# A fused attention layer on Trainium2: the per-layer embedding product computed before attention and kept in DRAM

## The chip, the core and the metric

The kernel runs on one core of one Trainium2 chip. A core has a matrix engine (PE, with its weight loads listed apart as PEld), a vector engine (DVE), a scalar engine (ACT), a general engine (POOL) and a queue engine that only issues transfers (SP). Each runs its own instruction list in order; they meet at semaphores. SP and POOL issue the transfers, which 16 DMA engines carry. The metric is the device time of one execution in microseconds, lower is better.

## What is computed

One layer over 512 tokens of width 2048. Cut to what matters here:

```python
hn = rmsnorm(x, norm_g)                            # 512 x 2048
x = x + swa_mixer(hn, w_in, w_out, sinks, rel_bias)  # windowed attention, 32 heads of 64, gated
emb = p @ ple_proj                                 # 512 x 256 times 256 x 2048
g = sigmoid(rmsnorm(x, ple_norm) @ ple_gate)       # 512 x 2048 times 2048 x 2048
x = x + emb * g
out = rmsnorm(x, final_g)
```

`p` and `ple_proj` are inputs: `emb` depends on nothing that the layer computes.

## The kernel before

Every float32 product is made of three matmuls on numbers split into a high and a low part (`mm3`, lines 123 to 128: high by high, high by low, low by high). A weight tile of 128x1024 arrives as `wraw` or `braw`, ACT makes the high part from it (`whi`, `bhi`), DVE the low part (`wlo`, `blo`). That pair of instructions is called a split below. Raw tiles and both parts have three buffers each.

The stages in order of time. **First projections** (lines 199 to 309): k, v and the first two q tiles. **Attention** (lines 852 to 941): 64 steps of softmax work, one every 5.6 us, between which PE makes the remaining 30 q and gate tiles. The generator `projections` yields after each product of three matmuls, seven or eight products fall into a step, and class `Weights` keeps its splits a few tiles ahead through a list `todo`, emptied at fixed points of a step. In the same steps `sum_weights` (line 686) prepares sums of weight blocks in DRAM for the later stages: SP issues a plain copy DRAM to DRAM (line 689), POOL later adds a second block into it (line 691). The first eight copies are issued at the end of step 0 (`sums_in`, line 883). **Output product** (lines 1107 to 1153) and **gate stage** (from line 1157): both use a Strassen scheme of seven half-size products, named by p, in two halves jj; class `Pieces` loads and splits their weight tiles. PE runs the gate stage in the order p = 2, 7, 1, 6, 5, 3, 4. The embedding is made there: for p = 1, 5, 3 each half loads a piece of `ple_proj` ("proj", split like a weight tile), and after the half's 48 matmuls `embed` (line 1165) makes two banks with six matmuls each; p = 4 is made block by block by `block` (line 1299, tiles named `last`), each block followed by six embedding matmuls, the last block in two halves of 256 columns. `gated` (line 1171) then multiplies the sigmoid with the embedding bank, adds to x and squares.

Order of the engines: PE and SP follow the program text everywhere. DVE, ACT and POOL do so from line 340 until the end of attention and again from the second product of the gate stage on (line 1258); between them a scheduler orders them. So code that is written elsewhere is issued elsewhere, and an instruction that waits holds up all behind it on its engine.

Of the kernel before, what the change touches and what calls it, by code (L numbers as in the profile page):

```python
# [55 lines left out]
def trunk_kernel(ctx: ExitStack, tc: tile.TileContext, a: dict):  # L56
# [31 lines left out]
    class Weights:  # L88


        def __init__(self, ahead):
            self.srcs, self.ahead, self.raw, self.made = [], ahead, [], []

            self.todo, self.asked, self.apart = [], 0, False

        def add(self, src):
            self.srcs.append(src)
# [1 line left out]
        def load(self, upto):  # L99
            for i in range(len(self.raw), upto):  # L100
                self.raw.append(wpool.tile([P, WE], F32, tag="wraw", name=f"wraw{i}"))
                nc.sync.dma_start(self.raw[i], self.srcs[i])

        def _make(self, i):
            self.load(min(i + 2, len(self.srcs)))
            raw = self.raw[i]
            hi = wpool.tile([P, WE], F32R, tag="whi", name=f"whi{i}")
            lo = wpool.tile([P, WE], F32R, tag="wlo", name=f"wlo{i}")
            nc.scalar.copy(hi, raw)  # L109
            nc.vector.tensor_sub(lo, raw, hi.bitcast(F32))  # L110
            self.made.append(tuple(t.rearrange("p (k c) -> p k c", k=8) for t in (hi, lo)))
# [77 lines left out]
    for kind, c in kinds:  # L189
# [470 lines left out]
    def block(nm, r, c, jj, m):  # L660
        return a[nm][2 * (c - 1) + jj, 4 * (r - 1) + m]

    SUMS = [("w_out", 7), ("w_out", 5), ("w_out", 6), ("w_out", 4), ("ple_gate", 7), ("ple_gate", 5)]

    def small_block(r, c, m):
# [27 lines left out]
    class Pieces:  # L693
# [9 lines left out]
        def _prepare(self, i):  # L703
            kind, src, key = self.specs[i]
            if kind == "grow":
                t = self.grown[key]
                nc.gpsimd.dma_start(t, src, accum_op=ALU.add)  # L707
            else:
                if kind == "seed":
# [10 lines left out]
                nc.sync.dma_start(t.rearrange("p (k c) -> p k c", k=2) if kind == "proj" else t, src)  # L720
            self.base[i] = t

        def _split(self, i):
            raw = self.base.pop(i)
            hi = wpool.tile([P, WE], F32R, tag="whi", name=f"bhi{i}")
            lo = wpool.tile([P, WE], F32R, tag="wlo", name=f"blo{i}")
            nc.scalar.copy(hi, raw)  # L727
            nc.vector.tensor_sub(lo, raw, hi.bitcast(F32))  # L728
            self.made[i] = tuple([t[:, :512], t[:, 512:]] for t in (hi, lo))
# [36 lines left out]
    def add_stage(nm, order):  # L766
        at = {}

        def add_embeds(p, jj):
            if nm == "ple_gate" and p in (1, 5, 3, 4):  # L770
                j = jj + 2 * (p in (5, 3))
# [80 lines left out]
    def projections():  # L852
        parts = {}
        for m, (kind, c) in enumerate(kinds):

            while any(v in chores for v in parts.get(m - 2, ())):
                chores.pop(0)()
            ps = bank(f"{kind}ps{c}", "p")
            for k in range(KC):
                if m == len(kinds) - 1 and k % 8 == 0:  # L860
                    B.ahead(k // 8 - 2)
                if m == len(kinds) - 1 and 2 <= k:
                    next(first_form, None)
                wh, wl = W.get(2 * m + k // 8)
# [8 lines left out]
    nc.scalar.mul(sinkb, sinkb, -1.0)  # L873
    proj = projections()
    load_bias(0)
    W.apart = True
    for n in range(KC):
        next(proj)
        if n % 4 == 3 and W.todo:
            W.todo.pop(0)()  # L880
    blocks = TWOS * UNITS

    def sums_in(i):
# [67 lines left out]
    pTh = late.tile([P, 2, S], F32R, name="pTh")  # L951
    pTl = late.tile([P, 2, S], F32R, name="pTl")
    ssq2 = const.tile([P, NB, 4], F32, name="ssq2")
    ssq3 = const.tile([P, NB, 5], F32, name="ssq3")

# [200 lines left out]

    rstd2 = const.tile([P, NB], F32, name="rstd2")
    ss2 = const.tile([P, NB], F32, tag="sums", name="ss2")
    pT = wpool.tile([P, WE], F32, tag="wraw", name="pT").rearrange("p (k t) -> p k t", k=2)
    nc.sync.dma_start(pT, a["pT"])  # L1160
    nc.scalar.copy(pTh, pT)
    nc.vector.tensor_sub(pTl, pT, pTh.bitcast(F32))
    done = {t: 0 for t in range(NB)}

    def embed(t, w, tag, c=slice(0, 512)):
        e_ps = bank(f"e{t}_{done[t]}", tag)
        for k in range(2):
            mm3(e_ps[:, c], pTh[:, k, blk(t)], pTl[:, k, blk(t)], w[0][k][:, c], w[1][k][:, c], k == 0, k == 1)
        return e_ps

    def gated(t, j, zin, z, e_ps, c=slice(0, 512)):


        n = done[t]
# [1 line left out]
        xt = x1[j][:, t, c]  # L1176
        nc.scalar.activation(z, zin, AF.Sigmoid, scale=rstd2[:, t : t + 1])
        yield
        nc.vector.tensor_mul(z, e_ps[:, c], z)
        if t >= 2 and j >= 2:  # L1180
            nc.gpsimd.dma_start(xt, z, accum_op=ALU.add)
        else:
# [72 lines left out]
    for n, p in enumerate(ORDER_PLE[:-1]):  # L1255
# [8 lines left out]
        for jj in range(2):  # L1264
# [31 lines left out]
    w = [B.get(at_ple["e", jj]) for jj in range(2)]  # L1296
    f = ple_forms.made[4]

    def block(jj, tb, tag, e_tag, c=slice(0, 512)):

        ps = bank(f"last{jj}_{tb}_{c.start}", tag)
        for k in range(8):
            fh, fl = f[k // 2]
            bh, bl = B.made[at_ple[4, jj][k // 2]]
            mm3(ps[:, c], fh[:, k % 2, blk(tb)], fl[:, k % 2, blk(tb)], bh[k % 2][:, c], bl[k % 2][:, c], k == 0, k == 7)
        e_ps = embed(2 + tb, w[jj], e_tag, c)
        z = s2[:, jj, tb, c]

        def opened():
            nc.vector.tensor_sub(z, ps[:, c], z)  # L1310
            return gated(2 + tb, jj, z, z, e_ps, c)

        return opened

# [14 lines left out]
    g = block(0, 0, "s", "o")()  # L1329
    run(root)  # L1330
    for step in moved.pop():
        step()
# [6 lines left out]
    for j in range(4):  # L1339
        row(1, j, yn2[:, 1:2])  # L1340
        store(1, j)
    g = block(1, 0, "s", "t")()
    next(g)
    for j in (2, 3):
        by_gain(2, j)
# [7 lines left out]
    g = block(0, 1, "p", "o")()  # L1353
    run(root)
    next(g)
    for j in range(2):
# [10 lines left out]
    g = block(1, 1, "p", "t", slice(0, 256))()  # L1367
    next(g)
    by_gain(3, 0)
    next(g)  # L1370
    run(g)
    n = done[3]
    last = block(1, 1, "s", "o", slice(256, 512))()
    next(last)

    nc.vector.tensor_reduce(base, ssq3[:, 3, :n], axis=AX.X, op=ALU.add)
# [83 lines left out]
```

## Time and profile before

| what | value |
|---|---|
| median of 3 runs | 794.62 us (794.57 to 794.85) |
| the profiled execution's own time | 794.82 us |
| span from its first to its last instruction | 793.1 us |
| PE busy | 783.2 us, 99% |
| DVE, ACT, POOL busy | 585.7, 506.7, 148.5 us |
| mean granted clock of PE | 0.997 |
| moved by DMA | 185.23 MB |

The rows of a timeline have the start in us from the span's beginning, the duration, engine, line, operation, the tile written and the tiles read, the shape, and in brackets how long the engine was idle before it and what ended that. A matmul's listed duration overlaps the next one's, so the distance between two starts is what PE spends on one. A row of a table by stretches has the stretch, its length, the busy time of PE, PEld, DVE, ACT and POOL with their counts, the granted clock, the DMA engines' busy share and GB/s.

### The profile page before, as it was taken

How to read it: one execution, taken by the hardware profiler on the slowest of the kernel's cores; microseconds unless marked ns; L12 is line 12 of the kernel's file. 1: busy time of each engine (PE TensorE's matmuls, PEld its weight loads, DVE VectorE, ACT ScalarE, POOL GpSimd, SP SyncE). 2: the span in 40 equal slices, each digit the busy share in tenths (PEclk: the TensorE clock that was granted, in tenths of full speed). 3: DMA queues.
4: the chain of work that ended last, by engine and by line, in shares of the span. 5: the costliest groups of instructions: out<-in, count | busy, mean ns of one | idle time of the engine just before them, and what ended most of it. 6: DMA issues, size and time to landing. Idle time of an engine off the chain costs nothing.

```text
span 793.1 us, 11181 instructions
## 1 busy us (share of the span) xinstructions
PE 783.2 (99%) x3746; PEld 656.0 (83%) x3746; DVE 585.7 (74%) x1155; ACT 506.7 (64%) x1067; POOL 148.5 (19%) x248
## 2 busy tenths in 40 slices
PE   9999999999999999999999999999999999999995
PEld 8888888888888888888888888888888888888885
DVE  4547587867867587767777899778866757988896
ACT  6743576666767586766666654466699656656765
POOL 0200423242413324132324200000000120210000
PEclk9999999999999999999999999999999999999998
DMA  9977999897989989898987498667864996787533
GB/s 349 275 215 264 207 275 303 223 267 215 277 227 269 223 249 258 230 247 235 244 227 182 140 365 337 197 212 232 275 237 142 346 203 202 157 225 220 176 107 106
DMA packets 45066, 185.23 MB, mean 234 GB/s; under 512 B 6656, under 2 KB 7680, under 8 KB 39888
## 3 DMA queue, kind: packets, MB, share of 16 engines
q1 hardware_dynamic: 36928, 143.30, 53.0%
q0 software_dynamic: 8080, 41.22, 27.1%
q8 instruction: 29, 0.48, 0.2%
q14 instruction: 29, 0.24, 0.1%
HBM read 177.63 MB, written 62.97 MB: 303 GB/s over the span
## 4 chain that ended last, share of the span: by engine, by line
PE 99%; DVE 0%; ACT 0%; ACTq 0%; issue 0%; DVEq 0%
PE gps L126 7%; PE gps L127 7%; PE gps L128 7%; PE qps L126 7%; PE qps L127 7%; PE qps L128 7%; PE o L127 6%; PE g L128 6%; PE g L127 5%; PE o L126 5%; PE o L128 5%; PE g L126 5%; PE s L477 2%; PE o L583 2%; PE vps L290 2%; PE pt L541 2%
## 5 line engine op out<-in xcount | busy, mean ns | idle before, releaser
L728 DVE TENSOR_TENSOR blo<-braw,bhi 128x1024 fp32r<-128x1024 f32 x102 | 124.4, 1222 | 40.9 <-ACT bhi L727 40.6
L727 ACT CAST bhi<-braw 128x1024 fp32r<-128x1024 f32 x102 | 107.3, 1052 | 72.2 <-PE o L128 24.8
L126 PE MATMUL gps<-xh,whi 128*128 128x512 f32 x256 | 100.0, 390 | 0.0
L127 PE MATMUL gps<-xl,whi 128*128 128x512 f32 x256 | 99.9, 390 | 0.0
L128 PE MATMUL gps<-xh,wlo 128*128 128x512 f32 x256 | 99.8, 390 | 0.0
L126 PE MATMUL qps<-xh,whi 128*128 128x512 f32 x224 | 87.8, 392 | 0.0
L127 PE MATMUL qps<-xl,whi 128*128 128x512 f32 x224 | 87.4, 390 | 0.0
L128 PE MATMUL qps<-xh,wlo 128*128 128x512 f32 x224 | 87.3, 390 | 0.0
L110 DVE TENSOR_TENSOR wlo<-wraw,whi 128x1024 fp32r<-128x1024 f32 x60 | 73.7, 1229 | 6.1 <-ACT whi L109 5.9
L547 DVE TENSOR_TENSOR r<-pt,r 128x256 fp32r<-128x256 f32 x64 | 27.2, 424 | 66.5 <-ACT r L546 65.6
L546 ACT CAST r<-pt 128x256 fp32r<-128x256 f32 x64 | 23.9, 373 | 80.9 <-PE pt L541 80.8
L126 PE MATMUL g<-bhi,fhg 128*128 128x512 f32 x192 | 75.1, 391 | 0.0
L126 PE MATMUL o<-bhi,fho 128*128 128x512 f32 x192 | 74.8, 390 | 0.0
L128 PE MATMUL g<-bhi,flg 128*128 128x512 f32 x192 | 74.8, 389 | 0.0
L127 PE MATMUL o<-blo,fho 128*128 128x512 f32 x192 | 74.8, 389 | 0.0
L128 PE MATMUL o<-bhi,flo 128*128 128x512 f32 x192 | 74.7, 389 | 0.0
L127 PE MATMUL g<-blo,fhg 128*128 128x512 f32 x192 | 74.7, 389 | 0.0
L557 POOL TENSOR_SCALAR_AFFINE_SELECT own<-r 64x512 fp32r<-64x512 f32 (+1 forms) x48 | 32.5, 677 | 224.6 <-DVE r L547 208.7
L109 ACT CAST whi<-wraw 128x1024 fp32r<-128x1024 f32 x60 | 62.2, 1039 | 5.4 <-issue 4.0
L492 POOL COPY t<-sinkb 128x2 f32<-128x2 f32 x64 | 53.2, 839 | 57.7 <-ACT sinkb L873 32.4
L707 POOL DMA_DIRECT2D grown<-in_ple_gate x16 | 13.8, 861 | 231.0 <-DVE blo L728 226.7
L128 PEld LDWEIGHTS gps<-xh,wlo 128*128 128x128 f32 x256 | 48.1, 188 | 10.3
(228 smaller groups left out, 1800.3 us busy)
## 6 DMA issues: line engine op xcount, KB each, us to landing
wraw<-in_w_gate_in SPq DMA_DIRECT2D x32, 512.0 KB, 6.5
w_out<-in_w_out POOLq DMA_DIRECT2D x32, 512.0 KB, 8.0
braw<-w_out SPq DMA_DIRECT2D x32, 512.0 KB, 4.4
wraw<-in_w_q SPq DMA_DIRECT2D x28, 512.0 KB, 5.3
braw<-in_ple_gate SPq DMA_DIRECT2D x24, 512.0 KB, 4.1
braw<-in_w_out SPq DMA_DIRECT2D x22, 512.0 KB, 4.2
xw<-in_first SPq DMA_DIRECT2D x14, 640.5 KB, 6.4
w_out<-in_w_out SPq DMA_DIRECT2D x16, 512.0 KB, 10.1
```

Of the source, the lines that this page charges most:

```text
L109: nc.scalar.copy(hi, raw)
L110: nc.vector.tensor_sub(lo, raw, hi.bitcast(F32))
L126: nc.tensor.matmul(ps, sh, mh, start=first, stop=False, skip_group_check=more)
L127: nc.tensor.matmul(ps, sh, ml, start=False, stop=False, skip_group_check=more)
L128: nc.tensor.matmul(ps, sl, mh, start=False, stop=last, skip_group_check=more)
L290: nc.tensor.matmul(v_ps[t], h[:, c], part_of(high_at, 256, 512), start=f, stop=e, skip_group_check=True)
L492: nc.gpsimd.tensor_copy(two(0, W + W - 1 if late else W, 1), sinkb[:, d : d + 1].unsqueeze(1).to_broadcast([P, 2, 1]))
L546: nc.scalar.copy(rh, src)
L547: nc.vector.tensor_sub(rl, src, rh.bitcast(F32))
L557: nc.gpsimd.affine_select(out=flat(own), in_=flat(r).bitcast(F32), pattern=[[0, 8], [sign, HB]], compare_op=ALU.is_ge, fill=0.0, base=-HB ...
L727: nc.scalar.copy(hi, raw)
L728: nc.vector.tensor_sub(lo, raw, hi.bitcast(F32))
```

## The change

All 16 products of `p @ ple_proj` are made in one stretch, between the first gate tile (g0) and step 0 of attention. `pT` and four pieces of `ple_proj` become entries 2 to 6 of `Weights`, so that later weight tiles have numbers higher by five; the split `pT` lives in a buffer of the tile `q`. ACT and DVE copy the banks to SBUF in pairs, POOL stores each pair to DRAM, in all eight of 512 KB. In the gate stage the pieces "proj" are replaced by pieces "made": they are loaded from DRAM and not split, and `gated` reads them in place of a bank.

```diff
         for n in range(2):
             W.add(a["w_gate_in" if kind == "g" else "w_q"][c][:, n * WE : (n + 1) * WE])
+        if m == 0:
+            W.add(a["pT"])
+            for j in range(4):
+                W.add(a["ple_proj"].rearrange("(k p) d -> p k d", p=P)[:, :, j * 512 : (j + 1) * 512])
...
+    def embed():
+
+        h, l = (v.rearrange("p k c -> p (k c)").rearrange("p (k t) -> p k t", k=2) for v in W.get(2))
+        for j in range(4):
+            wh, wl = (v.rearrange("p k c -> p (k c)").rearrange("p (k c) -> p k c", k=2) for v in W.get(3 + j))
+            for t in range(NB):
+                e_ps = bank(f"e{t}_{j}", "to"[t % 2])
+                for k in range(2):
+                    mm3(e_ps, h[:, k, blk(t)], l[:, k, blk(t)], wh[:, k], wl[:, k], k == 0, k == 1)
+                if t % 2 == 0:
+                    both = apool.tile([P, 2, S], F32, tag="u", name=f"both{t}_{j}", bufs=3)
+                    nc.scalar.copy(both[:, 0], e_ps)
+                else:
+                    nc.vector.tensor_copy(both[:, 1], e_ps)
+                    nc.gpsimd.dma_start(embedded[t // 2, j], both.rearrange("p b c -> p (b c)"))
+                if t == 1 and W.todo:
+                    W.todo.pop(0)()
+
+    embed()
     blocks = TWOS * UNITS
...
         def _split(self, i):
             raw = self.base.pop(i)
+            if self.specs[i][0] == "made":
+                self.made[i] = raw.rearrange("p (b c) -> p b c", b=2)
+                return
...
-                B.add("proj", a["ple_proj"].rearrange("(k p) d -> p k d", p=P)[:, :, j * 512 : (j + 1) * 512])
+                B.add("made", embedded[int(p in (5, 4)), jj + 2 * (p in (5, 3))])
...
-        nc.vector.tensor_mul(z, e_ps[:, c], z)
+        nc.vector.tensor_mul(z, e[:, c], z)
...
                 for t in (0, 1) if p in (1, 3) else (2, 3):
-                    e[t] = embed(t, w, "to"[jj])
+                    e[t] = w[:, t % 2]
...
-        e_ps = embed(2 + tb, w[jj], e_tag, c)
+        e = w[jj][:, tb]
```

What that does to SP's list at the start of attention, before (`wraw5` and `wraw6` are the second half of the fourth q tile and the first half of gate tile 1; `small` and `w_out` are the eight copies DRAM to DRAM; `DV` are differences of the values that step 5 first needs):

```order
L102 DMA wraw5_906<-in_w_q 128x1024
L689 DMA small_7_0_769<-in_w_out 16x8192
L689 DMA small_7_1_770<-in_w_out 16x8192
L689 DMA w_out_7_0_0_771<-in_w_out 16x8192
L689 DMA w_out_7_0_1_772<-in_w_out 16x8192
L689 DMA w_out_7_0_2_773<-in_w_out 16x8192
L689 DMA w_out_7_0_3_774<-in_w_out 16x8192
L689 DMA w_out_7_1_0_775<-in_w_out 16x8192
L689 DMA w_out_7_1_1_776<-in_w_out 16x8192
L102 DMA wraw6_1013<-in_w_gate_in 128x1024
L440 DMA DV_767<-diffs_899 64x512 x4
L102 DMA wraw7_1080<-in_w_gate_in 128x1024
```

and now, where `wraw10`, `wraw11` and `wraw12` hold what `wraw5`, `wraw6` and `wraw7` held:

```order
L105 DMA wraw9_1082<-in_w_q 128x1024
L700 DMA small_7_0_777<-in_w_out 16x8192
L700 DMA small_7_1_778<-in_w_out 16x8192
L700 DMA w_out_7_0_0_779<-in_w_out 16x8192
L700 DMA w_out_7_0_1_780<-in_w_out 16x8192
L700 DMA w_out_7_0_2_781<-in_w_out 16x8192
L700 DMA w_out_7_0_3_782<-in_w_out 16x8192
L700 DMA w_out_7_1_0_783<-in_w_out 16x8192
L700 DMA w_out_7_1_1_784<-in_w_out 16x8192
L105 DMA wraw10_1140<-in_w_q 128x1024
L105 DMA wraw11_1195<-in_w_gate_in 128x1024
L450 DMA DV_767<-diffs_1075 64x512 x4
```

The copies stand behind `wraw9` now, which reuses the buffer of `wraw6`, a piece of `ple_proj`; the load that stood ahead of them stands behind them.

The splits of the new stretch on DVE (`both0_1` is the copy of a pair's second bank; `wlo4` to `wlo7` are the low parts of the next pieces, `wlo6` that of the last piece of `ple_proj`):

```order
L916 COPY both0_0_902<-e1_0_904 128x512
L116 TENSOR_TENSOR wlo4_916<-wraw4_876,whi4_915 128x1024
L916 COPY both2_0_926<-e3_0_928 128x512
L916 COPY both0_1_944<-e1_1_946 128x512
L116 TENSOR_TENSOR wlo5_958<-wraw5_913,whi5_957 128x1024
L916 COPY both2_1_968<-e3_1_970 128x512
L916 COPY both0_2_986<-e1_2_988 128x512
L116 TENSOR_TENSOR wlo6_1000<-wraw6_955,whi6_999 128x1024
L916 COPY both2_2_1010<-e3_2_1012 128x512
```

Before, `wlo3` was followed at once by the softmax of step 0 there; now each piece is split behind the second bank of the piece before it.

At the end of the gate stage DVE had, before (`blo116` and `blo117` are splits of `ple_proj`, `z` and `e` the sigmoids and embedding banks of p = 3, `low6` and `low7` low parts for p = 4):

```order
L728 TENSOR_TENSOR blo115_7530<-braw115_7483,bhi115_7529 128x1024
L1179 TENSOR_TENSOR z0_0_7501<-e0_2_7469,z0_0_7501 128x512
L1183 TENSOR_TENSOR x1s_5004<-x1s_5004,z0_0_7501 128x512
L1179 TENSOR_TENSOR z0_1_7502<-e1_2_7476,z0_1_7502 128x512
L1183 TENSOR_TENSOR x1s_5004<-x1s_5004,z0_1_7502 128x512
L728 TENSOR_TENSOR blo116_7550<-braw116_7503,bhi116_7549 128x1024
L736 TENSOR_TENSOR low6_7567<-grown76_6583,last5_7523 128x1024
L728 TENSOR_TENSOR blo117_7571<-braw117_7527,bhi117_7570 128x1024
L1179 TENSOR_TENSOR z1_0_7588<-e0_3_7574,z1_0_7588 128x512
```

and now:

```order
L752 TENSOR_TENSOR low5_7610<-grown75_6737,last5_7609 128x1024
L1208 TENSOR_TENSOR z0_0_7587<-emb110_7462,z0_0_7587 128x512
L1212 TENSOR_TENSOR x1s_5186<-x1s_5186,z0_0_7587 128x512
L1208 TENSOR_TENSOR z0_1_7588<-emb110_7462,z0_1_7588 128x512
L1212 TENSOR_TENSOR x1s_5186<-x1s_5186,z0_1_7588 128x512
L752 TENSOR_TENSOR low6_7645<-grown76_6759,last5_7609 128x1024
L1208 TENSOR_TENSOR z1_0_7648<-emb115_7569,z1_0_7648 128x512
```

The three splits are gone and the rest keeps its order. On PE, all 102 matmuls named `e` leave the gate stage, among them the six of 256 columns that were PE's last instructions, and 96 of 512 columns stand between g0 and step 0.

More of the change, by code (lines that the diff above doesn't have):

```diff
@@ L92, in __init__ @@
             self.srcs, self.ahead, self.raw, self.made = [], ahead, [], []
-            self.todo, self.asked, self.apart = [], 0, False
+            self.todo, self.asked, self.apart, self.places = [], 0, False, {}
         def add(self, src):
@@ L101, in load @@
                 self.raw.append(wpool.tile([P, WE], F32, tag="wraw", name=f"wraw{i}"))
-                nc.sync.dma_start(self.raw[i], self.srcs[i])
+                to = self.raw[i]
+                if len(self.srcs[i].shape) == 3:
+                    to = to.rearrange("p (k c) -> p k c", k=2)
+                nc.sync.dma_start(to, self.srcs[i])
         def _make(self, i):
@@ L106, in _make @@
             raw = self.raw[i]
-            hi = wpool.tile([P, WE], F32R, tag="whi", name=f"whi{i}")
-            lo = wpool.tile([P, WE], F32R, tag="wlo", name=f"wlo{i}")
+            if i in self.places:
+                hi, lo = self.places[i]()
+            else:
+                hi = wpool.tile([P, WE], F32R, tag="whi", name=f"whi{i}")
+                lo = wpool.tile([P, WE], F32R, tag="wlo", name=f"wlo{i}")
             nc.scalar.copy(hi, raw)
@@ L188, in trunk_kernel @@
             g += 1
-    for kind, c in kinds:
+    for m, (kind, c) in enumerate(kinds):
         for n in range(2):
             W.add(a["w_gate_in" if kind == "g" else "w_q"][c][:, n * WE : (n + 1) * WE])
+        if m == 0:
+            W.add(a["pT"])
+            for j in range(4):
+                W.add(a["ple_proj"].rearrange("(k p) d -> p k d", p=P)[:, :, j * 512 : (j + 1) * 512])
     kvq = mid.enter_context(tc.tile_pool(name="kvq", bufs=1))
@@ L661, in block @@
         return a[nm][2 * (c - 1) + jj, 4 * (r - 1) + m]
+    embedded = {(u, j): tc.dram_tile([P, WE], F32, name=f"embedded{u}_{j}") for u in range(2) for j in range(4)}
     SUMS = [("w_out", 7), ("w_out", 5), ("w_out", 6), ("w_out", 4), ("ple_gate", 7), ("ple_gate", 5)]
@@ L708, in _prepare @@
             else:
-                if kind == "seed":
+                if kind == "made":
+                    t = rooms[0].tile([P, WE], F32, tag="made", name=f"emb{i}", bufs=2)
+                elif kind == "seed":
                     t = self.grown[key] = rooms[0].tile([P, WE], F32, tag="grown", name=f"grown{i}", bufs=8)
@@ L719, in _prepare @@
                         t = wpool.tile([P, WE], F32, tag="wraw", name=f"braw{i}")
-                nc.sync.dma_start(t.rearrange("p (k c) -> p k c", k=2) if kind == "proj" else t, src)
+                nc.sync.dma_start(t, src)
             self.base[i] = t
@@ L863, in projections @@
                     next(first_form, None)
-                wh, wl = W.get(2 * m + k // 8)
+                wh, wl = W.get(2 * m + k // 8 + (5 if m else 0))
                 mm3(ps, wh[:, k % 8, :], wl[:, k % 8, :], xh[k], xl[k], k == 0, k == KC - 1)
@@ L873, in trunk_kernel, with in_q @@
     nc.scalar.mul(sinkb, sinkb, -1.0)
+    def in_q():
+        room = kvq.tile([P, S // QB, 4, QB], F32R, tag="q", name="pTs", bufs=2).rearrange("p s h q -> p (s h q)")
+        return room[:, :WE], room[:, WE:]
+    W.places[2] = in_q
     proj = projections()
@@ L880, in trunk_kernel @@
             W.todo.pop(0)()
+    def embed():
[9 more added lines that the diff above has]
+                    nc.scalar.copy(both[:, 0], e_ps)
+                else:
+                    nc.vector.tensor_copy(both[:, 1], e_ps)
[3 more added lines that the diff above has]
+    embed()
     blocks = TWOS * UNITS
@@ L950, in trunk_kernel @@
     fg = late.tile([P, D], F32, name="fg")
-    pTh = late.tile([P, 2, S], F32R, name="pTh")
-    pTl = late.tile([P, 2, S], F32R, name="pTl")
     ssq2 = const.tile([P, NB, 4], F32, name="ssq2")
@@ L1158, in trunk_kernel, with gated @@
     ss2 = const.tile([P, NB], F32, tag="sums", name="ss2")
[L1159 to L1162, printed above, removed]
     done = {t: 0 for t in range(NB)}
[L1165 to L1171, printed above, removed]
+    def gated(t, j, zin, z, e, c=slice(0, 512)):
         n = done[t]
@@ L1310, in opened @@
             nc.vector.tensor_sub(z, ps[:, c], z)
-            return gated(2 + tb, jj, z, z, e_ps, c)
+            return gated(2 + tb, jj, z, z, e, c)
         return opened
@@ L1372, in trunk_kernel @@
     n = done[3]
-    last = block(1, 1, "s", "o", slice(256, 512))()
+    last = block(1, 1, "s", slice(256, 512))()
     next(last)
```

11 lines of the change are left out of this document (5 added, 6 removed).

## The prediction

> **What bounds the kernel now.** I read the page's busy times first, then the list of what PE waits for, then timelines of PE at the two places where the change acts. The page and that list:
>
> ```profile
> span 793.1 us, 11181 instructions
> PE 783.2 (99%) x3746; PEld 656.0 (83%) x3746; DVE 585.7 (74%) x1155; ACT 506.7 (64%) x1067; POOL 148.5 (19%) x248
> ...
> PE warm_ps L141 <- PEq L1450: 0.8, 1, 0.8
> ```
>
> The last row (waiter, releaser, us in all, times, longest) is the only wait of PE in the whole span: 0.8 us at the start. PE is the bound, without a gap, until its last instruction; what follows is a tail of some 9 us on DVE, ACT and the store. So the change cannot win by removing a wait, only by removing PE's work or shortening the tail. The question is what new waits it makes.
>
> **The work of PE** stays, it only moves. The last microseconds of the gate stage, PE's and DVE's part of it:
>
> ```profile
> 775.29 0.39 PE L126 MATMUL e<-bhi,pTh 128*128 128x512 f32 x1
> 775.49 0.69 DVE L1310 TENSOR_TENSOR s<-last,s 128x512 f32<-128x512 f32 x1 [0.36 <-PE last L128]
> 776.65 0.28 PE L126 MATMUL last<-last,fhg 128*128 128x256 f32 x1
> ...
> 783.00 0.28 PE L128 MATMUL last<-last,flg 128*128 128x256 f32 x1
> 783.12 0.28 PE L126 MATMUL e<-bhi,pTh 128*128 128x256 f32 x1
> 783.32 0.43 DVE L1310 TENSOR_TENSOR s<-last,s 128x256 f32<-128x256 f32 x1 [0.78 <-PE last L128]
> 783.72 0.28 PE L128 MATMUL e<-bhi,pTl 128*128 128x256 f32 x1
> 783.78 0.51 ACT L1177 ACTIVATE s<-s,rstd 128x256 f32<-128x256 f32 x1 [2.82 <-DVE s L1310]
> 784.32 0.42 DVE L1179 TENSOR_TENSOR s<-e,s 128x256 f32<-128x256 f32 x1
> ```
>
> Six embedding matmuls of 512 columns take 776.65 − 775.29 = 1.36 us, 0.227 each; one of 256 columns takes 783.12 − 783.00 = 0.12.
>
> ```profile
> L126 PE MATMUL e<-bhi,pTh 128*128 128x512 f32 (+1 forms) x34 | 12.8, 377 | 0.0
> ```
>
> The row counts 34 of them on one of three lines, so 102: 12 of 256 columns (two half blocks of six) and 90 of 512. Now there are 96 of 512. **Term 1.** Before, the last six stand behind the last `last` matmul, and beside them run the subtraction of L1310 (783.32) and the sigmoid (783.78) that L1179 (784.32) needs anyway: those 0.72 us cost nothing. Up to the last `last` matmul PE has 90 x 0.227 + 6 x 0.12 = 21.15 us of embedding work before and 96 x 0.227 = 21.79 now. If nothing else changed, the end would move by **+0.64 us**.
>
> **Term 2: the end of the gate stage.** DVE loses six splits of `ple_proj` there, but the tail's work does not shrink with PE's. The two stretches are p = 5 and 3 (first half's start to the first multiplication of p = 3's second half) and from there to the last subtraction; columns as in the section on the profile:
>
> ```profile
> 703.14:757.78 54.64, 54.64 (x243) 45.24 (x242) 47.40 (x52) 38.03 (x51) 3.44 (x4) 1.00 0.63 195
> 757.78:783.32 25.54, 25.54 (x140) 22.27 (x140) 23.06 (x49) 14.93 (x27) 0.00 (x0) 1.00 0.38 124
> ...
> 713.62 1.22 DVE L736 TENSOR_TENSOR spare<-grown,spare 128x1024 fp32r<-128x1024 f32 x1
> 714.75 1.22 DVE L728 TENSOR_TENSOR blo<-braw,bhi 128x1024 fp32r<-128x1024 f32 x1
> ...
> 753.53 0.39 PE L126 MATMUL e<-bhi,pTh 128*128 128x512 f32 x1
> 756.33 1.25 ACT L1177 ACTIVATE z<-g,rstd 128x512 f32<-128x512 f32 x2
> 757.78 0.68 DVE L1179 TENSOR_TENSOR z<-e,z 128x512 f32<-128x512 f32 x1
> ```
>
> A split holds DVE 714.75 − 713.62 = 1.13 us. In the first stretch DVE comes to 47.40 − 6 x 1.13 = 40.6 us, and PE, without three pairs of banks, needs (753.53 − 703.14) − 3 x 2.72 = 42.2: PE still sets the pace, just. In the tail it turns. Behind 753.53 PE has three blocks of 24 matmuls at 0.227 and one of 48 halves at 0.12, 16.3 + 5.8 = 22.1 us. DVE has 25.54 us from its first L1179 to its last L1310, and only the 0.36 and 0.78 us in brackets at 775.49 and 783.32 are waits for PE, which go away: 24.4 us remain. It can start when the sigmoid of a finished product is there, one of 512 columns takes 1.25 / 2 = 0.63 us at 756.33, and with the 0.2 us between 783.12 and 783.32 for a drain that is about 0.9 us behind PE. 0.9 + 24.4 − 22.1 = **+3.2 us**. Bounds: if all of DVE's idle time (25.54 − 23.06 = 2.48) went, it would be 0.9 + 23.06 − 22.1 = 1.9; if DVE started as late behind PE as ACT's sigmoids do in the trace (756.33 + 0.63 − 753.53 = 3.4) but with the same chain, 3.4 + 24.4 − 22.1 = 5.7. I take 3.2 since ACT loses a cast there and DVE a split, which is what put the sigmoids so late. The e matmuls were the slack that hid this work of DVE; without them DVE is late next.
>
> **The stretch itself.** PE, SP and DVE at the place where it is put:
>
> ```profile
> 81.68 0.33 SPq L102 DMA_DIRECT2D wraw<-in_w_gate_in  x1
> 82.36 0.33 PE L477 MATMUL s<-k,q 128*128 128x64 f32 x2
> ...
> 79.89 1.75 DVE L110 TENSOR_TENSOR wlo<-wraw,whi 128x1024 fp32r<-128x1024 f32 x1
> ...
> x1s<-in_x POOLq DMA_DIRECT2D x2, 1024.0 KB, 6.7
> ```
>
> Attention's first matmul is at 82.36; the 96 new ones go there: 96 x 0.227 = 21.8 us, to 104.1. A piece j takes a quarter of it, 5.44 us, a pair of banks 2.72. Each piece needs one split (DVE 1.22 by the page's row below, 1.75 at 79.89 when POOL works beside it) and two bank copies of about 0.7 us (as L1310's 0.69): some 3.2 of 5.44 us on DVE. A pair's buffer is one of three, so a store of 512 KB has 2 x 2.72 = 5.4 us and more; the trace has one of 1024 KB issued by POOL that landed in 6.7 us. I cost the stretch at **0**; if a store takes the whole 6.7 us the second and later rounds wait up to 2 us in all.
>
> **Term 3: what stands behind the stretch on SP.**
>
> ```profile
> 65.24 0.84 SPq L102 DMA_DIRECT2D wraw<-in_w_q  x2
> 66.13 1.29 SPq L689 DMA_DIRECT2D small<-in_w_out  x2
> 67.46 4.62 SPq L689 DMA_DIRECT2D w_out<-in_w_out  x6
> ...
> 91.61 0.58 SPq L102 DMA_DIRECT2D wraw<-in_w_gate_in  x1
> ...
> L728 DVE TENSOR_TENSOR blo<-braw,bhi 128x1024 fp32r<-128x1024 f32 x102 | 124.4, 1222 | 40.9 <-ACT bhi L727 40.6
> ```
>
> Before, SP issues the eight copies DRAM to DRAM from 66.13 to 72.08, 16 us before attention. Now they stand behind `wraw9`, whose buffer is free when `wraw6` is split, and that split stands behind the second bank of the third piece (pieces j = 0 to 3): 82.36 + 2 x 5.44 + 2.72 = 95.96 on PE, then a drain (0.2), a copy (0.6) and the split (1.22): 98. So the copies start 32 us later while attention moves by 21.8: they come **10.2 us closer** to it, and the loads behind them with them. Has DMA room there? Attention's first 24 us, and the loads' times to landing in a view of the stretch 88 to 92:
>
> ```profile
> 84.00:104.00 20.00, 20.00 (x98) 16.71 (x97) 12.60 (x35) 11.91 (x35) 4.82 (x8) 1.00 1.01 220
> 104.00:108.00 4.00, 4.00 (x20) 3.31 (x19) 3.72 (x12) 3.76 (x12) 0.81 (x2) 1.00 0.57 166
> ...
> DV<-diffs SPq DMA_DIRECT2D x4, 128.0 KB, 10.4
> wraw<-in_w_gate_in SPq DMA_DIRECT2D x1, 512.0 KB, 12.9
> ...
> 105.11 1.05 ACT L109 CAST whi<-wraw 128x1024 fp32r<-128x1024 f32 x1
> 106.83 0.40 ACT L567 CAST own<-own 64x256 fp32r<-64x256 f32 x1
> 109.24 0.28 PE L585 MATMUL o<-own,DV 128*128 128x256 f32 x1
> ```
>
> The DMA engines are full from 84 to 104 (share 1.01), and the backlog is gone only after 104 (0.57, so 0.43 x 4 = 1.7 us of room). The load issued at 91.61 landed 12.9 us later, at 104.5, and its cast on ACT starts 0.6 us after, at 105.11. [...] So a landing 10.2 us later is met by 1.7 us of room, 0.6 us before the cast and about 1.6 before PE: PE waits 10.2 − 1.7 − 0.6 − 1.6 = 6.3, and I take **+6.0 us** with the rounding of the steps. From both sides: 0 when the copies and POOL's adds, which share these engines, are spread more widely by the stretch's 22 us, and 10.2 when all of the delay reaches PE.
>
> **The sum**: 0.64 + 3.2 + 0 + 6.0 = 9.85 us on the profiled execution's 794.82, 804.67; the median stands 0.2 under that execution, so **804.5 us**.
>
> **Rivals.** *A, the loads are in time.* For it: the stretch has few loads of its own (pT and four pieces, 2.5 MB, and 4 MB of stores), and the page shows DMA share falling after 104. Against it: the five full rows before. Terms 1 and 2 remain: 794.62 + 3.84 = 798.5. *B, not slower: PE still sets the end.* If DVE's tail is made of waits for ACT that vanish with the splits, it is shorter than PE's; it decides below 22.1 − 0.9 = 21.2 us of DVE work. DVE's busy time of 23.06 speaks against it. With the loads in time only term 1 is left: 795.3. *C, PE's wait costs twice.* The forecast puts PE's loss in one stretch; if it idles for long in one piece the granted clock falls with it:
>
> ```profile
> 785.00:790.00 5.00, 0.00 (x0) 0.00 (x0) 2.73 (x10) 2.60 (x6) 0.00 (x0) 0.84 0.35 128
> 790.00:793.00 3.00, 0.00 (x0) 0.00 (x0) 0.00 (x0) 0.00 (x0) 0.00 (x0) 0.50 0.37 139
> ```
>
> PE's last matmul starts at 783.72 and is done at 784.0. The clock's mean of 0.84 over 785 to 790 is 0.50 for 0.16 / 0.5 = 32% of 5 us, so it fell at 788.4: 4.4 us after PE stopped. If PE waits longer than that in one piece, say 8 us of the 10.2, and the clock needs as long to come back (an estimate: the trace does not show a return), 4.4 us at half pace lose 2.2 us: 0.64 + 3.2 + 8 + 2.2 = 14.0, **808.7**.
>
> [...]
>
> **Chances.** The forecast, with a PE wait of 2 to 8 us in attention's first steps and DVE last in the tail: 0.60. A: 0.17. B: 0.08. C: 0.13. Faster: 0.01, since PE's work of 783 us stays and nothing waits now; 0.01 for anything else. What a measurement of this kernel tells from no change is about 0.2%, 1.6 us; B lies within it, the others above. So faster 0.01, same 0.08, slower 0.91. The range of 8 in 10 leaves out B and the upper part of C: from A with term 2 at its lower bound, 794.62 + 0.64 + 1.9 = 797.2, to 810.0, where C stands with term 2 somewhat above 3.2.
>
> **What would show it.** In the profile of the changed kernel: no PE wait between 82 and 104 (the stretch costs nothing); the copies' issue at about 98 instead of 66 on SP; PE waiting between about 125 and 145 for `own`, DV or a high part, 6 us in sum (term 3), with the granted clock below 1 there only by C; in the tail the last subtraction on DVE starting some 3 us after PE's last matmul with no PE in its brackets (term 2), and the rest of the tail as long as before. I am wrong if PE's list of waits stays empty (A), or if DVE's last subtraction still waits for PE (B). A faster time would show as fewer microseconds of PE than 783, which nothing here provides.

## The result: 812.54 us, and where it went

The changed kernel takes 812.54 us (median of 4 runs, 812.36 to 815.24), the kernel before 794.62 (794.57 to 794.85): a ratio of 1.0233, 95% interval 1.0211 to 1.0254. It is slower, as forecast, but by 17.9 us and not by 9.9, and 812.54 lies above the range's upper end of 810.0. One execution of the run e5_diff_first below, the profiled one, had a granted clock of 0.75 and took 984.54 us; it is left out, and no wait is read from its profile.

The profiled execution after has a span of 810.6 us (its own time 812.36), 17.5 more than before. The page's first lines, and the list of what PE waits for (waiter, releaser, us in all, times, longest):

```profile
span 810.6 us, 11215 instructions
PE 785.4 (97%) x3740; PEld 655.6 (81%) x3740; DVE 585.1 (72%) x1159; ACT 506.8 (63%) x1071; POOL 150.9 (19%) x256
...
PE o L595 <- ACT own L577: 9.5, 1, 9.5
PE warm_ps L147 <- PEq L1479: 0.8, 1, 0.8
PE s L487 <- DVE sm L520: 0.5, 1, 0.5
PE g L133 <- DVE blo L744: 0.5, 1, 0.5
```

One wait of 9.5 us stands out, and nothing in the list lies in the stretch itself (82 to 104). PE, ACT and the load behind the wait, from the timeline and from the view of transfers at the load's issue:

```profile
97.61 1.24 SPq L700 DMA_DIRECT2D small<-in_w_out  x2
...
115.10 0.34 SPq L105 DMA_DIRECT2D wraw<-in_w_gate_in  x1
...
wraw<-in_w_gate_in SPq DMA_DIRECT2D x1, 512.0 KB, 23.5
...
138.66 1.04 ACT L115 CAST whi<-wraw 128x1024 fp32r<-128x1024 f32 x1 [8.35 <-DMA wraw<-in_w_gate_in]
...
140.38 0.40 ACT L577 CAST own<-own 64x256 fp32r<-64x256 f32 x1
...
140.83 0.58 PE L595 MATMUL o<-own,DV 128*128 128x256 f32 x1 [9.52 <-ACT own L577]
142.18 0.63 PE L133 MATMUL gps<-xl,whi 128*128 128x512 f32 x1
142.60 0.63 PE L134 MATMUL gps<-xh,wlo 128*128 128x512 f32 x1
143.88 0.39 PE L134 MATMUL gps<-xh,wlo 128*128 128x512 f32 x1
144.10 0.39 PE L132 MATMUL gps<-xh,whi 128*128 128x512 f32 x1
```

The list names ACT's cast of `own`; the reader is to look one step behind it. ACT itself waits 8.35 us for a weight load, and `own` stands behind the cast of that load. The load was issued at 115.10 and took 23.5 us, where the same load took 12.9 before. Then the clock: PE's matmuls are 0.42 us apart at 142.18 and 0.22 apart from 143.88 on. Stretches of the same profile (columns as in the section on the profile before):

```profile
104.00:124.00 20.00, 20.00 (x95) 16.61 (x94) 10.36 (x33) 10.79 (x29) 10.68 (x20) 1.00 1.01 332
124.00:144.00 20.00, 9.97 (x42) 7.85 (x41) 10.74 (x29) 8.01 (x25) 1.45 (x4) 0.74 0.90 225
```

PE is busy for half of 124 to 144, at a mean clock of 0.74. And the end, PE's last matmul and DVE's last subtraction:

```profile
796.59 0.28 PE L134 MATMUL last<-last,flg 128*128 128x256 f32 x1
...
801.12 0.42 DVE L1339 TENSOR_TENSOR s<-last,s 128x256 f32<-128x256 f32 x1
```

Before, these two stood at 783.00 and 783.32. PE's last `last` matmul comes 13.6 us later, DVE's subtraction now 4.53 us behind it and not 0.32: 4.2 us more. What follows the subtraction is 0.3 us shorter (793.1 − 783.32 against 810.6 − 801.12). 13.6 + 4.2 − 0.3 = 17.5.

Of the 13.6 us, the distances between PE's starts put 12.1 into attention's first steps (10.3 at the two long gaps, 1.5 at half clock, the rest scattered), 0.64 is the added work of term 1, 1.5 lie in two places where the low part of a split was late (near 504 and 708); the rest, 0.7 us less, lies mostly in the span's first microseconds.

### The profile page after: what moved, and what is told of

The parts are those of the page before. It is cut to its first block, busy times and chain, and to the rows that moved or that the text cites. A ratio compares the mean times of both kernels' runs of the same rounds, so it can differ in the third digit from the quotient of the medians.

```text
span 810.6 us, 11215 instructions
## 1 busy us (share of the span) xinstructions
PE 785.4 (97%) x3740; PEld 655.6 (81%) x3740; DVE 585.1 (72%) x1159; ACT 506.8 (63%) x1071; POOL 150.9 (19%) x256
## 4 chain that ended last, share of the span: by engine, by line
PE 84%; DVE 6%; DMA 6%; ACT 2%; issue 1%; SPq 1%; ACTq 0%; DVEq 0%
PE gps L132 7%; PE gps L133 7%; PE gps L134 7%; PE qps L132 6%; PE qps L133 6%; PE qps L134 6%; PE g L133 5%; PE g L134 5%; PE g L132 5%; PE o L133 5%; PE o L134 5%; PE o L132 5%; DMA wraw<-in_w_gate_in 3%; PE s L487 2%; PE vps L300 2%; PE o L593 2%
## 5 line engine op out<-in xcount | busy, mean ns | idle before, releaser
L744 DVE TENSOR_TENSOR blo<-braw,bhi 128x1024 fp32r<-128x1024 f32 x94 | 114.5, 1222 | 36.9 <-ACT bhi L743 36.6
L743 ACT CAST bhi<-braw 128x1024 fp32r<-128x1024 f32 x94 | 98.8, 1052 | 67.6 <-PE o L134 22.9
L116 DVE TENSOR_TENSOR wlo<-wraw,whi 128x1024 fp32r<-128x1024 f32 x65 | 79.2, 1220 | 19.5 <-ACT whi L115 19.5
L115 ACT CAST whi<-wraw 128x1024 fp32r<-128x1024 f32 x65 | 67.5, 1040 | 14.3 <-DMA wraw<-in_w_gate_in 9.8
```

## The experiments

The question was why attention's start lost 12.1 us and not 6, and whether the tail's 4.2 us are what the prediction said. Theory: the eight copies DRAM to DRAM come late and crowd the loads. Rivals: the 4 MB of stores crowd them; or something else that the stretch holds up. PE's idle times below are from each kernel's profiled execution.

### The copies ahead of the stretch

```diff
+    for n in range(0, SUMS_EARLY, 2):
+        sum_weights(n)
     embed()
...
         if i == 0:
-            return range(0, SUMS_EARLY, 2)
+            return range(0)
```

> The changed kernel with the eight copies DRAM to DRAM emitted ahead of the embedding stretch, so that they are issued near 66 us again. Theory (the copies, held behind wraw9 until 98 us, crowd the loads of attention's first steps): the PE wait for own (9.5 us) and the fall of the clock behind it are gone; left are 0.64 us of PE work and some 4.2 us of DVE in the tail and two short waits for blo: about 800.5 us (799 to 802). Rival (the 4 MB of stores crowd the loads, wherever the copies stand): a PE wait of 4 us or more stays between 120 and 145, 805 us or more.

Measured: 804.18 us (803.07 to 805.32), ratio 1.0124 (1.0109 to 1.0139). The copies are issued from 64.82 on and 8.4 us are back, but not all: the wait for `own` is now three waits.

```profile
PE o L595 <- ACT own L577: 4.6, 3, 1.9
...
104.68 0.53 POOL L917 DMA_DIRECT2D embedded<-both  x1 [2.17 <-ACT whi L115]
...
109.39 1.68 POOL L702 DMA_DIRECT2D small<-in_w_out  x2
...
wraw<-in_w_gate_in SPq DMA_DIRECT2D x1, 512.0 KB, 14.3
```

By the wait (over 4 us) this is the rival's result, by the time (below 805) neither's. The rows point to a third cause, which the later runs test. POOL's last store is at 104.68; only then come the differences that attention needs and the adds into the sums, from 109.39. Before, the adds began ahead of attention:

```profile
82.19 1.68 POOL L691 DMA_DIRECT2D small<-in_w_out  x2
```

82.19 is 0.2 us ahead of attention's start at 82.36; 109.39 is 6.1 us behind it, since attention starts at 103.26 in this run. So the five first adds, 512 KB each, came 6.3 us nearer to attention's loads and fall on those of DV and `wraw12`.

### No stores

The eight stores left out (the gate stage reads blocks of `ple_gate` instead), the copies late as in the change:

```diff
-                    nc.gpsimd.dma_start(embedded[t // 2, j], both.rearrange("p b c -> p (b c)"))
```

> The changed kernel without the eight stores of the stretch: the products are made and copied but not stored, and the gate stage reads blocks of ple_gate of the same size in their place, so the output lacks the embedding. Theory (the late copies are the larger part, the stores add to the backlog): the copies are still issued at about 98 us, the landing of wraw12 comes some 4 to 7 us earlier than 138.6, the PE wait for own falls from 9.5 to between 2 and 6 us: 804 to 808 us. Rival (the stores alone are the cause): no PE wait, about 800.5. Other rival (the stores cost nothing): wait and time stay, 812.5.

Measured: 809.84 us (808.73 to 810.84), ratio 1.0195 (1.0179 to 1.0210). Only 2.7 us are gained, less than the theory expected and far from the rival's 800.5. The wait for `own` is short, but another load is late in its place, and behind that wait the clock is low:

```profile
PE qps L132 <- ACT whi L115: 3.5, 1, 3.5
...
PE o L595 <- ACT own L577: 0.8, 1, 0.8
...
124.00:144.00 20.00, 18.35 (x75) 14.61 (x76) 16.03 (x40) 14.78 (x40) 2.38 (x5) 0.83 0.96 255
```

With the low clock taken as the 0.50 that the changed kernel's profile has from 134.00 to 143.88, the mean of 0.83 is half pace for 0.17 / 0.5 = 34% of 20 us, 6.8 us, and PE works in nearly all of them (18.35 of the 20): an estimate of some 3 us lost, twice the 1.5 of the changed kernel. So PE's waits here shrink by more than the time does. The adds are issued at 104.72, when the late copies have landed, and not at 109.49 as in the changed kernel. With the copies late, it takes no stores to lose most of the time.

### The kernel before with late copies

The kernel before, with the copies moved behind `wraw6` on SP, and the first five adds moved with them (issued from 88.48 on POOL and not from 82.19); the place of the copies:

```diff
+                if i == 2:
+                    for v in range(0, SUMS_EARLY, 2):
+                        sum_weights(v)
```

> The kernel before, with nothing changed but the place of the eight copies on SP: behind wraw6, the first load of attention's steps, so that they are issued from about 82 us on and not 66. No embedding is moved. Theory (copies close to attention's loads are enough): wraw7 lands 8 to 16 us later than 104.5, PE waits for own 6 to 13 us near 110, 802 to 811 us. Rival (the loss needs the stretch and its stores): wraw7 lands within 4 us of 104.5, PE waits less than 3 us, 794.6 to 797.5.

Measured: 805.64 us (804.65 to 806.42), ratio 1.0138 (1.0121 to 1.0155). The list of PE's waits, the transfer of `wraw7`, issued at 94.94, and a stretch:

```profile
PE o L585 <- ACT own L567: 8.8, 1, 8.8
...
wraw<-in_w_gate_in SPq DMA_DIRECT2D x1, 512.0 KB, 21.1
...
104.00:124.00 20.00, 11.19 (x44) 9.09 (x43) 7.75 (x23) 7.34 (x19) 2.38 (x5) 0.74 0.89 238
```

The load lands at 116.0, 11.6 us later than before, the same wait arises at the same instruction, and the clock falls to the same mean: without one embedding matmul moved. Copies close to attention's loads, with the adds that wait for them, are enough.

### Matmuls put back into the tail

The copies ahead, and six matmuls that nobody reads behind each block of the tail, where the embedding's stood:

```diff
+        fill = bank(f"fill{jj}_{tb}_{c.start}", "ot"[jj])
+        for k in range(2):
+            mm3(fill[:, c], fh[:, k, blk(tb)], fl[:, k, blk(tb)], bh[k][:, c], bl[k][:, c], k == 0, k == 1)
```

> e1_copies_first with matmuls that nobody reads put back where the embedding matmuls of p = 4 stood before: six behind each block of the tail, 18 of 512 columns and 12 of 256. They add 18 x 0.227 + 6 x 0.12 = 4.8 us of PE work ahead of the last matmul of the last block and 0.72 us behind it. Theory (DVE sets the end of the tail and is 4.2 us late behind PE): the time is that of e1_copies_first + 0.3 to 0.9. Rival (PE sets the end): + 4.8 us.

Measured: 804.40 us (803.72 to 805.61), 0.2 above e1_copies_first, far within the scatter of both. PE's last `last` matmul and DVE's last subtraction:

```profile
794.04 0.28 PE L134 MATMUL last<-last,flg 128*128 128x256 f32 x1
...
794.36 0.42 DVE L1344 TENSOR_TENSOR s<-last,s 128x256 f32<-128x256 f32 x1 [0.51 <-PE last L134]
```

4.8 us of PE work ahead of the last subtraction cost nothing: DVE, not PE, sets the end of the changed tail, and the matmuls just fill its lateness (the bracket shows PE late again, by 0.51).

### The first difference ahead of the stores

```diff
+    make_diff(1)
     embed()
...
-        if step == 0 and i < NB - 1:
+        if step == 0 and 1 <= i < NB - 1:
```

> e1_copies_first with the first difference of the values (L441, L442 on POOL) emitted ahead of the stretch too, so that POOL does it before its eight stores. Theory (what e1_copies_first still loses comes from POOL's list: the stores hold the differences, and so the five first adds are issued at 109.4 to 114.8, 5.4 us nearer to the loads of attention's first steps than before): the adds come about 1.6 us earlier, PE waits for own shrink from 4.6 us to 3 or so, 802 to 803.8 us. Rival (the 4 MB of stores on the DMA engines do it, wherever the adds stand): within 0.5 us of e1_copies_first.

Measured: 802.96 us (802.87 to 803.35), ratio 1.0105 (1.0089 to 1.0120). It lies where the theory put it, but its interval overlaps that of e1_copies_first, and the shorter wait that the theory names is not shown: one difference is too little to tell anything.

### The first adds ahead of the stores

```diff
     make_diff(1)
+    for n in range(7, SUMS_EARLY, 2):
+        sum_weights(n)
     embed()
```

> e5_diff_first with the five first adds emitted ahead of the stretch as well: they are issued as the copies land, from 72 to 84 us, ahead of the first store. The stores stay. Theory (POOL's order put the adds onto attention's loads): the PE waits between 120 and 160 go, 5.7 us less than e1_copies_first, about 798.5 us (797.5 to 799.5); left are 0.64 us of PE work and the tail on DVE. Rival (the stores crowd the loads): the waits stay above 3 us, 802 or more.

Measured: 810.87 us (808.62 to 811.34), ratio 1.0199 (1.0185 to 1.0212): 12 us off the expectation, and in the wrong direction. The waits between 120 and 160 are gone, as the theory said, but PE now stops inside the stretch:

```profile
PE e L132 <- ACT both L914: 6.5, 1, 6.5
...
79.41 1.70 POOL L702 DMA_DIRECT2D small<-in_w_out  x2
...
embedded<-both POOLq DMA_DIRECT2D x3, 512.0 KB, 14.4
```

The adds start at 79.41, since POOL's differences need the values first. The stores behind them land after 14.4 us. Three `both` buffers cover little more than 5.4; then ACT cannot copy the next bank (at 102.00 it has waited 11.1 us for a store), and PE waits for the bank.

### Rows of the tail on POOL and ACT

On top of the kernel above, the rows t = 0 and 1 are multiplied by the gain on POOL and scaled on ACT:

```diff
+    for t in range(2):
+        for j in range(4):
+            nc.gpsimd.tensor_mul(x1[j][:, t, :], x1[j][:, t, :], gain(j))
...
-        row(0, j, yn2[:, 0:1])
+        nc.scalar.mul(x1[j][:, 0, :], x1[j][:, 0, :], yn2[:, 0:1])
```

> e6_adds_first with eight instructions of DVE taken out of the tail: the rows t = 0 and 1 (L1233, 0.69 us each, 5.5 in all) are multiplied by the gain on POOL and scaled on ACT, both idle for much of the tail. Theory (DVE is 4.2 us late behind PE there): DVE is no longer last, the last subtraction starts 0.3 to 1 us behind PE's last matmul, 3.5 to 4 us less than e6_adds_first, about 795. Rival (the lateness is in waits for ACT and not in DVE's work, or POOL slows DVE): less than 1.5 us gained, or none.

Measured: 814.29 us (813.32 to 815.22), slower than e6_adds_first by 3.4 us. DVE's last subtraction is still 4.86 us behind PE, and PE waits 2.3 us for the low part of a split at one more place. While POOL multiplies (1.5 us for each), some of DVE's tiny instructions become slow:

```profile
781.47 6.02 POOL L1358 TENSOR_TENSOR x1s<-x1s,fg 128x512 f32<-128x512 f32 x4
...
785.05 1.21 DVE L181 TENSOR_TENSOR t_r<-t_r,ms_r 128x2 f32<-128x2 f32 x1
```

In the changed kernel, where POOL does nothing in the tail, the same instruction took 0.16 us (at 782.00). A low part (L752) took 2.32 us at 780.28, beside POOL, and 1.22 at 775.46, when POOL was idle. So the run took work from DVE and made other work of DVE's longer, and it says nothing on DVE's share of the lateness; the run without rows below does.

### The first adds later

e5_diff_first with the first five adds moved to attention's steps 4 to 8:

```diff
-        if i < 4:
-            return range(4 * i + 3, min(4 * i + 7, SUMS_EARLY), 2)
...
+        late = [2 * i - 1] if 4 <= i < 9 else []
```

> e5_diff_first with the five first adds moved later, one in each of attention's steps 4 to 8, beside the adds that are there. Theory (DMA time is short around attention's start, and the adds stand on the loads of its first steps): the waits of PE near 130 go, and as attention's later steps have DMA shares of 0.92 to 1.02 too, a part of them comes back later: 798.5 to 802 us. Rival (the adds don't matter there): the waits near 130 stay, 803.

Measured: 802.74 us (802.41 to 806.40), ratio 1.0112 (1.0095 to 1.0129). The load of `wraw12`, issued at 114.80, its stretch, and PE's wait:

```profile
wraw<-in_w_gate_in SPq DMA_DIRECT2D x1, 512.0 KB, 3.7
...
104.00:124.00 20.00, 20.00 (x94) 16.63 (x94) 14.08 (x41) 13.37 (x36) 5.00 (x13) 1.00 0.61 173
...
PE o L595 <- ACT own L577: 1.4, 2, 0.9
```

All eight stores are there, and the load lands 3.7 us after its issue, not 14.3: it was the adds that POOL had been made to issue late, not the stores' traffic alone. PE loses 2.2 us between 140 and 180 instead, where the adds now are. Against e5_diff_first the time hardly moves (0.2 us): the transfer time is paid in another place.

### The first adds between the stores

```diff
                     nc.gpsimd.dma_start(embedded[t // 2, j], both.rearrange("p b c -> p (b c)"))
+                    if 2 * j + t // 2 < 5:
+                        sum_weights(7 + 2 * (2 * j + t // 2))
```

> e5_diff_first with the five first adds issued between the stores of the stretch, one behind each of the first five. Theory (one stock of DMA time: ahead of the stretch the adds held the last piece of ple_proj, behind it attention's loads; between them the shares of 0.79 in 84 to 104 leave some 4 us): no wait in the stretch, and the waits near 130 shrink from some 3 or 4 us to 0 to 2: 798.5 to 801 us. Rival (adds in the stretch delay its stores or pieces as they did ahead of it): PE waits above 3 us between 84 and 110, 803 or more.

Measured: 807.98 us (807.28 to 808.51), ratio 1.0167 (1.0154 to 1.0181): the rival's result. The stores land after 10.3 us, and PE waits in and right behind the stretch, where the clock's mean is 0.83 (104 to 124):

```profile
PE qps L132 <- ACT whi L115: 2.6, 1, 2.6
...
PE e L133 <- DVE wlo L116: 0.8, 1, 0.8
...
embedded<-both POOLq DMA_DIRECT2D x5, 512.0 KB, 10.3
```

### The copies ahead and no stores

e1_copies_first without the stores, by the same edit as above.

> e1_copies_first without the eight stores: the gate stage reads blocks of ple_gate of the same size in place of the embedding, so the output lacks the embedding. Theory (the late copies and the stores, with what they hold on POOL, are together the whole loss at attention's start): PE waits below 1 us between 80 and 160, about 798.5 us, e1_copies_first - 5.5. Rival (the loads of the stretch, 2.5 MB, or its place on ACT and DVE, cost by themselves): PE waits of 2 us or more stay, 800.5 or more.

Measured: 800.79 us (800.15 to 800.91), ratio 1.0077 (1.0064 to 1.0091). PE's whole list, and a row of POOL:

```profile
PE warm_ps L147 <- PEq L1480: 0.8, 1, 0.8
PE g L133 <- DVE blo L744: 0.5, 1, 0.5
PE o L133 <- DVE blo L744: 0.2, 1, 0.2
...
81.75 1.68 POOL L702 DMA_DIRECT2D small<-in_w_out  x2
```

No wait is left at attention's start, as the theory said, though the time lies where the rival put it; the number in the expectation was too low, since it was taken from a profiled execution that was 1.1 us above its kernel's median and forgot the two short waits. With no stores ahead of them on POOL the adds are issued from 81.75 on again, now some 22 us ahead of attention. What remains over the kernel before, 6.2 us, is the part of the change that does not lie at attention's start: 0.64 + 4.2 + 1.5 = 6.3.

### Rows left out

e1_copies_first without the eight multiplications of the rows t = 0 and 1, which are stored unscaled.

> e1_copies_first without the eight multiplications of the rows t = 0 and 1 by the gain and the root (L1233 on DVE, 0.69 us each): these rows are stored unscaled. Theory (DVE's work makes the tail 4.2 us late behind PE): with 5.5 us less of it the last subtraction starts 0.3 to 1 us behind PE's last matmul, and the time is 3.5 to 4.2 us below e1_copies_first. Rival (DVE waits for ACT's chain there, its own work is not what is late): less than 1.5 us.

Measured: 800.59 us (800.04 to 801.26), ratio 1.0077 (1.0063 to 1.0091), 3.6 us below e1_copies_first.

```profile
788.66 0.28 PE L134 MATMUL last<-last,flg 128*128 128x256 f32 x1
790.21 0.42 DVE L1341 TENSOR_TENSOR s<-last,s 128x256 f32<-128x256 f32 x1
```

The lateness falls from 4.5 to 1.55 us, 3.0 for 5.5 us of work, and not to the 0.3 to 1 us expected; the rest of the 3.6 is a shorter wait in attention, which this edit does not touch. DVE's own work is what is late, though not every microsecond of it counts. The trace shows what keeps the last 1.55: DVE has caught up with PE at 783.23, and its chain for the last block takes the 7.0 us from there to 790.21, with only 0.45 of waiting (for ACT), against 5.8 us of matmuls.

## Why the prediction was wrong

**PE's work and the stretch: right.** PE was the bound, its work only moved, and the 96 matmuls cost no wait where they stand: PE's list has none between 82 and 104, while the copies were issued at 97.61 (98 was forecast). Term 1, +0.64, is contained in the 6.2 us that e10_copies_first_no_stores leaves; no run measured it alone.

**Term 2, the tail: right in its mechanism, 1.0 us too small.** 4.2 us and not 3.2, within the bounds of 1.9 and 5.7. The part that was mis-sized is DVE's start behind PE, from PE's first matmul of the tail to DVE's first multiplication of p = 3's second half:

```profile
774.64 0.39 PE L132 MATMUL last<-spare,fhg 128*128 128x512 f32 x1
...
776.55 0.69 DVE L1208 TENSOR_TENSOR z<-emb,z 128x512 f32<-128x512 f32 x1
```

That is 1.9 us where 0.9 was taken: a cast for p = 4 on ACT (774.34) and its low part on DVE (775.41) still stood ahead of the sigmoid and the multiplication. DVE's chain from there to its last subtraction took 801.12 − 776.55 = 24.6 us (24.4 forecast), PE's matmuls 22.1 as forecast: 1.9 + 24.6 − 22.1 = 4.4, of which 0.2 were there before. In the two products ahead of the tail PE's sum was put too low, since PE starts p = 5 at 701.85 and not at 703.14, 43.5 us and not 42.2; that PE sets the pace there holds all the more. e4_copies_first_fill shows that PE has 4 us and more to spare in the tail, e11_no_rows that taking work from DVE brings the end forward. Rival B is dead by both.

**Not in the sum: 1.5 us** at 504 and 708, where PE reaches a split before its low part is made. At 708, DVE multiplies a pair of embedding banks just ahead of it. Before, PE had twelve embedding matmuls in that place, the first of them at 677.37, and first needed the low part behind them, at 680.32: the same lost cover as in the tail. The first row is of the kernel before, the others of the changed one:

```profile
677.37 0.39 PE L126 MATMUL e<-bhi,pTh 128*128 128x512 f32 x1
...
707.40 0.69 DVE L1212 TENSOR_TENSOR x1s<-x1s,s 128x512 f32<-128x512 f32 x1
708.01 1.22 DVE L744 TENSOR_TENSOR blo<-grown,bhi 128x1024 fp32r<-128x1024 f32 x1
```

This edge is the one from p = 1 to p = 6. The prediction compared DVE's sum with PE's only for the whole of p = 5 and 3 and did not look at it. The place at 504 is in the output product, which the change does not touch. There DVE starts a split late, behind a cast on ACT that waits for a load of `w_out`, and does not catch up (first row before, second row now):

```profile
461.65 1.05 ACT L727 CAST bhi<-braw 128x1024 fp32r<-128x1024 f32 x1 [2.57 <-DMA braw<-in_w_out]
...
496.25 1.05 ACT L743 CAST bhi<-braw 128x1024 fp32r<-128x1024 f32 x1 [4.10 <-DMA braw<-in_w_out]
```

PE is 33.1 us later there than before, this cast 34.6. Why the load lands 1.5 us later stays open.

**Term 3, what stands behind the stretch: the step that failed.** 6.0 us were forecast, with bounds of 0 and 10.2; it was 12.1. The chain was right to the instruction: late copies, a late load, the cast on ACT, `own`, PE. The term was mis-sized at one line, "a landing 10.2 us later is met by 1.7 us of room". It reckoned with the copies on SP's list alone, and costed the stretch's stores by their 0 to 2 us on PE. The stores stand on a second list. POOL's differences and adds were queued behind them and came some 6 us nearer to the loads that PE needs, and late copies and late adds then met in the same 20 us. With the prediction's 21.8 us for the stretch, the load landed 138.6 − 104.5 − 21.8 = 12.3 us late against attention, where 10.2 − 1.7 = 8.5 was reckoned; these 3.8 us and the clock's 1.5 (below) are most of what the term lacked. The 1.6 us of slack before PE are shown by no run: the rows before have 2.0 us from the end of `own`'s cast at 107.23 to PE's matmul at 109.24, and in the changed kernel the load's 12.3 us cost PE 10.3, so 2.0 us of slack in all where 0.6 + 1.6 were taken.

The runs part the two causes: with the copies alone put back 8.4 us return (e1_copies_first), and with the stores left out as well, so that the adds too are early again, another 3.4 (e10_copies_first_no_stores): together 11.8 of the 12.1. In the other order the same 11.8 us are 2.7 (e2_no_stores) and 9.0, so each counts for more where the other is gone. Leaving out the stores also takes 4 MB of transfers away. That the stores' traffic alone does not hold the load shows in e8_adds_later, where the load is in time with every store issued; that stores and adds do not fit together into the stretch either shows in e6_adds_first and e9_adds_between.

**Rival C came true beside it.** PE waited 9.52 us in one piece, and the clock fell: it is 0.50 from 134.00 to 143.88, and 1.5 us are lost in the 3.0 us from 140.83 to 143.88 in which PE ran at half pace. The prediction's estimate of 2.2 us took a return as long as the fall at the end of the span, 4.4 us. Neither length is the same from place to place. Here the fall came some 2.3 us after PE's stop at 131.31 (the clock's mean is 1.00 in 133.0 to 133.5, 0.62 in 133.5 to 134.0), and the return 3.0 us after PE's next matmul at 140.83; in e3_before_copies_late, behind a wait of nearly the same length, half pace lasted 4.7 us and cost 2.2.

```profile
118.27 0.58 PE L585 MATMUL o<-own,DV 128*128 128x256 f32 x1 [8.81 <-ACT own L567]
...
122.98 0.40 PE L126 MATMUL gps<-xh,whi 128*128 128x512 f32 x1
```

In e2_no_stores a wait of only 3.5 us cost some 3 us more at half pace, by the estimate above; in e1_copies_first, with three waits of 1.9 us at most, the clock's mean stays 1.00 from 124 to 164. So a long wait of PE had a second price here, and its size is not settled by the wait's length.

No order tried here makes the change worth its time. Even without any wait at attention's start it costs 6.2 us, since it takes PE work away from the place where it hid DVE's and puts it where PE was busy already.

## What to carry to other kernels

A kernel whose matrix engine never waits (0.8 us in all here) gains nothing from moving its work; but the work is cover for the other engines where it stands (4.2 us of DVE's in the tail), and what it covered has to be added up edge by edge before it goes. A stretch put into a program holds up every list on which it issues something: go through all of them, the one with its stores too, and look for what stood behind and had been running ahead. Here the transfer engines were nearly full on both sides of the stretch (busy shares of 0.91 in 64 to 84 and of 0.92 to 1.01 in 104 to 164 of e1_copies_first), and moving transfers moved the wait, as four places for the same five adds show: PE waited 4.6 us with them behind the stores (e1_copies_first), 6.5 ahead of the stores (e6_adds_first), 2.6 + 0.8 + 0.3 between them (e9_adds_between) and 1.4 with them in attention's later steps (e8_adds_later).

## What was not expected of the hardware

While one engine's queue of transfers held five adds of 512 KB, a store of 512 KB behind them took 14.4 us to land (e6_adds_first, median of three); with the same stores alone it took 4.2 (e1_copies_first, median of four):

```profile
embedded<-both POOLq DMA_DIRECT2D x4, 512.0 KB, 4.2
```

And two of DVE's instructions on two columns went from 0.16 and 0.17 us to 1.21 and 1.22 beside POOL's multiplications of 128x512 (e7_adds_first_rows); the tail that was to be relieved got no shorter.
